# Statistics of two RMSNorms as split float32r matmuls in a hybrid decoder layer

## The chip, the cores and the metric

The kernel runs on one core of one Trainium2 chip. The metric is the time of one launch in device microseconds (us). Before the change it is 837.26 us, the median of 3 runs (836.93 to 837.74).

## The reference

One decoder layer on 512 tokens of width 1024: a half-step SwiGLU feed-forward, a mixer (RG-LRU channels beside sliding-window attention), and a second half-step feed-forward. Each of the three is wrapped in an RMSNorm on its input (pre norm) and one on its output (post norm):

```python
def rms_norm(x, g):
    xf = x.astype(jnp.float32)
    y = xf * lax.rsqrt(jnp.mean(xf * xf, axis=-1, keepdims=True) + RMS_EPS)
    return (y * g.astype(jnp.float32)).astype(x.dtype)

x = x + 0.5 * rms_norm(swiglu(rms_norm(x, ffn1_pre_g), ffn1_w_gu, ffn1_w_down), ffn1_post_g)
y = hybrid_mixer(rms_norm(x, mix_pre_g), w_in, ...)
x = x + rms_norm(y, mix_post_g)
x = x + 0.5 * rms_norm(swiglu(rms_norm(x, ffn2_pre_g), ffn2_w_gu, ffn2_w_down), ffn2_post_g)
```

All inputs are float32. The change touches the pre norms with `mix_pre_g` and `ffn2_pre_g`: the mean over 1024 features of the squares, for each of the 512 tokens.

## The kernel before, in words

**Layout.** x lies feature-major: 8 tiles `xT[c]` of 128 features by 512 tokens. Every large product is made of float32r matmuls (a form of fp32 that the array takes as one matmul record; the trace prints its type as fp32r where an engine writes it). Since float32r keeps fewer bits, each operand is split in a high part (a rounded copy made by ACT) and a low part (what is left, a subtraction on DVE), and each product is three matmuls: high by high, high by low, low by high (`mm3`, L509).

**A pre norm.** The class `Next` (L635) prepares the input of the next product. The gain is multiplied in before the product; the factor 1/rms of each token is multiplied in after it, so the product need not wait for the statistics. `sum_squares` (L653) adds the squares of the 8 tiles into `acc` (128 by 512): ACT squares (L656, L658 through `square`, L542), DVE adds (L658). `stats` (L582) then needs, for each token, the sum of `acc` over 128 partitions times 1/1024. It takes four matmuls, one for each block of 128 tokens, with the block of `acc` as the stationary operand and a column `mean_d` of 1/1024 as the moving one, in plain fp32 (L585); the result is one column per block. `invert` (L588) takes the root on ACT (L592), the reciprocal on DVE (L593), and lays the reciprocals on the diagonals of two tiles, high and low (L594 to L598). `spread` (L600) multiplies them with a matrix of ones (L602) so that every partition has 1/rms of every token, and ACT copies the result to the tile R (L666).

**Where it stands in the order.** The order on all engines is written out by hand: each engine runs its instructions in the order of the program. `boundary` (L755) ends one sub-layer and starts the next. Near its end stand `W.fill(2)`, `nxt.sum_squares()` (L825), and then the rest of the first four weight blocks' matmuls (`k_high`, L826, and `k_low`, L827). After `boundary` comes the next product, `pk` for the mixer (L1565) and `pg` of chunk 2 for the second feed-forward (L1111): 24 matmuls, and after 12 of them (the hook at k = 4) the `stats` matmuls. `spread` comes behind the product.

**Weights.** A queue (`Weights`, L50) loads raw weights over SP's DMA queue, rounds them on ACT (`cast`, L210) and subtracts on DVE or POOL (`take_low`, L215), a few units ahead of their use; a raw buffer that both have read is loaded again.

**Buffers.** Scratch tiles from `wt` (L163) share a ring of 8 buffers, `acc` tiles a ring of 3, PSUM has 8 banks in turn. A ring's buffer is used again when its last reader is done.

**Who else uses `InvRmsRows`.** The norm of the LRU output (`lrms`, L1895) and, through a subclass, the first layer's pre norm.

Of the kernel before, what the change touches and what calls it, by code (L numbers as in the profile page):

```python
# [8 lines left out]
F32 = mybir.dt.float32  # L9
F32R = mybir.dt.float32r  # L10
# [5 lines left out]
P = 128  # L16
T = 512
NB = T // P
D = 1024
# [103 lines left out]
def tile_layer(ctx: ExitStack, tc: tile.TileContext, out: bass.AP, **ins: bass.AP):  # L123
    nc = tc.nc
    pe, dve, act, pool, sync = nc.tensor, nc.vector, nc.scalar, nc.gpsimd, nc.sync

    const = ctx.enter_context(tc.tile_pool(name="const", bufs=1))
# [14 lines left out]
    def bank(name):  # L142
        return psum.tile([P, T], F32, tag="bank", name=name)
# [19 lines left out]
    def wt(name, w=T, dt=F32):  # L163
        return tmp.tile([P, w], dt, tag="w", name=name, bufs=NW)
# [291 lines left out]
    for name, n in ROWS:  # L456
        if name in ("b_rg", "b_ig"):

            j = name == "b_ig"
# [14 lines left out]
    def filled(name, w, value):  # L474
        t = const.tile([P, w], F32, name=name)
        dve.memset(t, value)
        return t
# [2 lines left out]
    dve.memset(ones.bitcast(F32), 1.0)  # L480
    mean_d = filled("mean_d", 1, 1.0 / D)
    mean_c = filled("mean_c", 1, 1.0 / C)
    eps = filled("eps", 1, EPS)
    eps4 = filled("eps4", 1, 4 * EPS)
    dummy = const.tile([P, 1], F32, name="dummy")
# [30 lines left out]
    def product(w, xs, sl=ALL, name="", hooks=()):  # L516
        ps = bank(name)
        hooks = dict(hooks)
        for k, x in enumerate(xs):
            if k in hooks:  # L520
                hooks[k]()
            mm3(ps[:, sl], w, k, [t[:, sl] for t in x], k == 0, k == len(xs) - 1)
        return ps
# [16 lines left out]
    def square(src, sl, name, scale=1.0):  # L540
        sq = wt(f"sq_{name}")[:, sl]
        act.activation(sq, src, AF.Square, scale=scale)  # L542
        return sq
# [3 lines left out]
    class InvRms:  # L547


        def __init__(self, accs, mean, half, name, eps=eps):  # L550
            self.accs, self.mean, self.half, self.name, self.eps = accs, mean, half, name, eps

        def stats(self):
            self.ps = ps = bank(f"rms_{self.name}")
            for i in range(2):
                b = 2 * self.half + i
                for j, a in enumerate(self.accs):
                    pe.matmul(ps[:, i:i + 1], a[:, b * P:(b + 1) * P], self.mean, start=j == 0, stop=j == len(self.accs) - 1)
            self.invert(ps[:, :2])
# [16 lines left out]
    class InvRmsRows:  # L576


        def __init__(self, acc, mean, name):
            self.acc, self.mean, self.name = acc, mean, name  # L580

        def stats(self):  # L582
            self.ps = ps = bank(f"rms_{self.name}")
            for b in range(NB):
                pe.matmul(ps[:, b:b + 1], self.acc[:, b * P:(b + 1) * P], self.mean, start=True, stop=True)  # L585
            self.invert(ps[:, :NB])
# [48 lines left out]
    class Next:  # L635
# [17 lines left out]
        def sum_squares(self):  # L653
            for c in range(KD):
                if c == 0:
                    act.activation(self.acc, xT[c], AF.Square)  # L656
                else:
                    dve.tensor_add(self.acc, self.acc, square(xT[c], ALL, f"n{self.name}{c}"))  # L658

        def stats(self):  # L660
            self.rms.stats()
# [802 lines left out]
    for g, (f0, f1) in enumerate(GROUPS1):  # L1464
# [20 lines left out]
        for c in range(KD):  # L1485
# [18 lines left out]
            b = pair_banks[c] if c < 2 else product(W.take(), xs, name=f"ya{g}{c}")  # L1504
# [6 lines left out]
    def in_product(name, hooks=(), ahead=AHEAD):  # L1511
        return product(W.take(ahead), mx.xs, name=name, hooks=hooks)
# [81 lines left out]
    for j in range(4):  # L1594
        b = in_product(f"pq{j}")
# [70 lines left out]
    hl = us_  # L1666
# [473 lines left out]
```

## Time and profile before

| | before |
|---|---|
| median of 3 runs | 837.26 us |
| the profiled execution | 837.42 us |
| its span, first to last instruction | 835.6 us |
| granted TensorE clock | 0.998 |
| busy: PE / PEld / DVE / ACT / POOL | 827.5 / 704.3 / 732.7 / 518.8 / 165.9 us |

PE is TensorE's matmuls, PEld its weight loads, which overlap the matmuls; DVE is VectorE, ACT ScalarE, POOL GpSimd, SP the queue that issues DMAs. A record's end on PE is modelled, and records overlap: the step from one start to the next tells more than the length. In a row of the timeline stand the start, the length, the engine, the line, the operation, output and inputs, the shape, how many records were merged, and in brackets how long the engine idled before and who ended that. In a matmul's row "128*128 128x512" is the stationary shape and the moving shape.

### The profile page before, as it was taken

The numbers are of one execution on the slowest core, as the hardware profiler recorded it, in microseconds if no ns is written. First come the engines' busy times: TensorE is split into PE (matmuls) and PEld (weight loads), VectorE is DVE, ScalarE is ACT, GpSimd is POOL, SyncE is SP. The second block draws the span as 40 slices with busy tenths as digits, with TensorE's granted clock in tenths as the row PEclk, the third lists the DMA queues.
The fourth block names the chain that finished last, engine by engine and source line by source line (L and its number), as shares of the span: only waits on it lengthen the run. The fifth ranks groups of instructions, "written<-read, shape, count | busy, mean of one in ns | idle before, by whom it ended". The sixth has DMA issues, their size and how long they took to land.

```text
span 835.6 us, 11875 instructions
## 1 busy us (share of the span) xinstructions
PE 827.5 (99%) x4244; PEld 704.3 (84%) x4244; DVE 732.7 (88%) x1035; ACT 518.8 (62%) x806; POOL 165.9 (20%) x188
## 2 busy tenths in 40 slices
PE   9999999999999999999999999999999999999996
PEld 8988888888888898987788899888888888888885
DVE  4989799998989977888789689998999799898996
ACT  6656756676666654556897446545757677676562
POOL 2022000140320325414521052002005023032001
PEclk9999999999999999999999999999999999999999
DMA  7376408398595897522511140566339939769742
GB/s 253 103 272 231 151 12 308 89 266 259 128 260 179 187 282 244 170 79 93 167 42 51 51 130 23 126 176 253 118 110 243 311 91 256 234 156 259 301 141 101
DMA packets 121851, 144.22 MB, mean 173 GB/s; under 512 B 24184, under 2 KB 76736, under 8 KB 121280
## 3 DMA queue, kind: packets, MB, share of 16 engines
q1 hardware_dynamic: 107824, 112.91, 42.2%
q0 software_dynamic: 13824, 30.42, 16.6%
q8 instruction: 33, 0.54, 0.3%
q14 instruction: 26, 0.21, 0.1%
q10 hardware_dynamic: 144, 0.13, 0.0%
HBM read 100.45 MB, written 39.32 MB: 167 GB/s over the span
## 4 chain that ended last, share of the span: by engine, by line
PE 98%; DMA 1%; DVE 0%; SPq 0%; issue 0%; DVEq 0%
PE aa L999 10%; PE ab L999 10%; PE db L999 5%; PE da L999 5%; PE yaa L1390 3%; PE ba L999 3%; PE bb L999 3%; PE ya L1390 3%; PE yda L1390 2%; PE aa L929 1%; PE a_first L1260 1%; PE yab L1981 1%; PE yab L1979 1%; PE yab L1980 1%; PE wo L1905 1%; PE gt L512 1%
## 5 line engine op out<-in xcount | busy, mean ns | idle before, releaser
L1171 POOL DMA_DIRECT2D yr_a<-stage x36 | 31.6, 1020 | 176.5 <-ACT stage L1168 156.0
L1171 POOL DMA_DIRECT2D yp_b<-stage x42 | 36.5, 1065 | 146.8 <-ACT stage L1168 118.4
L1995 POOL DMA_DIRECT2D yp_b<-stage x8 | 4.3, 546 | 64.9 <-ACT stage L1994 64.4
L722 POOL TENSOR_TENSOR acca_r<-acca_r,sq_r 128x512 f32<-128x512 f32 x6 | 8.6, 1430 | 39.7 <-ACT sq_r L542 39.6
L530 PE MATMUL an<-xh_mx,whi_xl 128*128 128x256 f32 x64 | 15.9, 289 | 0.0
L531 PE MATMUL an<-xh_mx,wlo_xl 128*128 128x256 f32 x64 | 15.5, 283 | 0.0
L2098 POOL TENSOR_TENSOR last<-yp,grow 128x512 f32<-128x512 f32 x3 | 3.9, 1292 | 56.5 <-DVE yp L2088 56.5
L2095 ACT ACTIVATE ysq<-yp 128x512 f32<-128x512 f32 (+1 forms) x8 | 4.9, 607 | 15.7 <-DVE yp L2088 15.7
L512 PE MATMUL gt<-xh_mx,whi_gt 128*128 128x512 f32 x32 | 14.3, 446 | 0.0
L1427 POOL DMA_DIRECT2D yp_a<-zy x16 | 8.7, 554 | 25.0 <-DMA rows_a<-yr_a 16.7
L512 PE MATMUL pq<-xh_mx,whi_q 128*128 128x512 f32 x32 | 12.8, 401 | 0.0
L514 PE MATMUL gt<-xh_mx,wlo_gt 128*128 128x512 f32 x32 | 12.6, 394 | 0.0
L512 PE MATMUL pgb<-xh_f,whi_bg 128*128 128x512 f32 x32 | 12.6, 393 | 0.0
L513 PE MATMUL gt<-xl_mx,whi_gt 128*128 128x512 f32 x32 | 12.5, 391 | 0.0
L514 PE MATMUL pq<-xh_mx,wlo_q 128*128 128x512 f32 x32 | 12.5, 391 | 0.0
L514 PE MATMUL pgb<-xh_f,wlo_bg 128*128 128x512 f32 x32 | 12.5, 390 | 0.0
L514 PE MATMUL pub<-xh_f,wlo_bu 128*128 128x512 f32 x32 | 12.5, 390 | 0.0
L513 PE MATMUL pq<-xl_mx,whi_q 128*128 128x512 f32 x32 | 12.5, 390 | 0.0
L513 PE MATMUL pub<-xl_f,whi_bu 128*128 128x512 f32 x32 | 12.5, 390 | 0.0
L512 PE MATMUL pub<-xh_f,whi_bu 128*128 128x512 f32 x32 | 12.5, 390 | 0.0
L513 PE MATMUL pgb<-xl_f,whi_bg 128*128 128x512 f32 x32 | 12.5, 389 | 0.0
L1390 PE MATMUL ya<-whi_ad,hha 128*128 128x512 f32 x32 | 12.5, 389 | 0.0
(2038 smaller groups left out, 3414.3 us busy)
## 6 DMA issues: line engine op xcount, KB each, us to landing
yp_b<-stage POOLq DMA_DIRECT2D x50, 256.0 KB, 9.0
yr_a<-stage POOLq DMA_DIRECT2D x44, 256.0 KB, 9.6
h_a<-za SPq DMA_DIRECT2D x16, 256.0 KB
h_b<-zb SPq DMA_DIRECT2D x16, 256.0 KB
hxb<-h_b SPq DMA_DIRECT2D x16, 256.0 KB
hxa<-h_a SPq DMA_DIRECT2D x6, 512.0 KB
xn<-in_x SPq DMA_DIRECT2D x8, 256.0 KB
raw_ad<-in_ffn_w_down SPq DMA_DIRECT2D x2, 1024.0 KB
```

The lines of the kernel that those rows point to most:

```text
L512: pe.matmul(ps, hi[:, k, :], xh, start=start, stop=False)
L513: pe.matmul(ps, hi[:, k, :], xl, start=False, stop=False)
L514: pe.matmul(ps, lo[:, k, :], xh, start=False, stop=stop)
L530: pe.matmul(ps[:, sl], hi[:, k, :], xh, start=k == 0 and not goes_on, stop=False, skip_group_check=True)
L531: pe.matmul(ps[:, sl], lo[:, k, :], xh, start=False, stop=False, skip_group_check=True)
L722: eng.tensor_add(acc, acc, square(part, ALL, f"{self.name}{c}"))
L929: pe.matmul(o, w[:, k, js], x, start=first and i + j + k == 0, stop=k == 3 and i == 2, skip_group_check=True)
L999: pe.matmul(b[tb], x[:, blk], w[:, k, :], start=first and q + k + j == 0, stop=q + k == 2 and j == 2, skip_group_check=True)
L1171: pool.dma_start(o, st, accum_op=ALU.add)
L1260: pe.matmul(banks[j][:, HALF[0]], ws[j][part][:, k, :], n1.xs[k][xpart][:, HALF[0]], start=k == 0 and part == xpart, stop=stop and k == KD ...
L1390: pe.matmul(o, x[:, blk], a[:, k, :], start=start and j == 0, stop=stop and j == 2, skip_group_check=True)
L1427: (pool if q % 2 else sync).dma_start(chunks[32 * q:32 * (q + 1), :, i * P:(i + 1) * P], turned[32 * i:32 * (i + 1), :, q])
```

## The change

The sum of squares of the two pre norms gets a method `apart`, called at the end of `sum_squares`: ACT copies `acc` to a float32r tile (the high part) and DVE subtracts it from `acc` (the low part), both in tiles of the `wt` ring. `stats` then takes, for each block of 128 tokens, two float32r matmuls (high, then low, added in PSUM) with two equal columns of 1/1024 in place of one fp32 matmul with one column. The root reads every second column. The LRU norm and the first pre norm keep the old way. `mean_r` is a new constant of two columns, set once at the start.

```diff
     mean_d = filled("mean_d", 1, 1.0 / D)
     mean_c = filled("mean_c", 1, 1.0 / C)
+    mean_r = const.tile([P, 2], F32R, name="mean_r")
+    dve.memset(mean_r.bitcast(F32), 1.0 / D)
...
         def __init__(self, acc, mean, name):
-            self.acc, self.mean, self.name = acc, mean, name
+            self.acc, self.mean, self.name, self.two = acc, mean, name, None
+
+        def apart(self):
+
+            self.two = hi, lo = [wt(f"acc{i}_{self.name}", T, F32R) for i in "hl"]
+            act.copy(hi, self.acc)
+            dve.tensor_sub(lo, self.acc, hi.bitcast(F32))
 
         def stats(self):
             self.ps = ps = bank(f"rms_{self.name}")
+            if self.two:
+                for b in range(NB):
+                    for j, a in enumerate(self.two):
+                        pe.matmul(ps[:, 2 * b:2 * b + 2], a[:, b * P:(b + 1) * P], mean_r, start=j == 0, stop=j == 1)
+                self.invert(ps[:, 0:2 * NB:2])
+                return
             for b in range(NB):
                 pe.matmul(ps[:, b:b + 1], self.acc[:, b * P:(b + 1) * P], self.mean, start=True, stop=True)
             self.invert(ps[:, :NB])
...
                     dve.tensor_add(self.acc, self.acc, square(xT[c], ALL, f"n{self.name}{c}"))
+            self.rms.apart()
```

## The prediction

> **What bounds the kernel now.** I read the busy times first, then the chain that ended last, then the waits of PE.
>
> ```profile
> PE 827.5 (99%) x4244; PEld 704.3 (84%) x4244; DVE 732.7 (88%) x1035; ACT 518.8 (62%) x806; POOL 165.9 (20%) x188
> ...
> PE 98%; DMA 1%; DVE 0%; SPq 0%; issue 0%; DVEq 0%
> ```
>
> ```profile
> PE warm L1247 <- POOL ident masks.py:199: 1.4, 1, 1.4
> PE xtp L1195 <- DMA xn<-in_x: 0.4, 1, 0.4
> ```
>
> PE is busy for 827.5 of 835.6 us, the chain of work that ended last is PE for 98%, and PE's whole list of waits is 1.8 us at the start. So PE never waits in the two stages that the change touches. Time can change in two ways only: the statistics' own records on PE get cheaper or dearer, or a wait of PE appears where there is none. What ACT and DVE do more is free as long as PE finds its data.
>
> **The statistics on PE now.** The timeline of PE and of its weight loads around the mixer's statistics, and the records of line 585:
>
> ```profile
> 365.81 0.39 PE L512 MATMUL pk<-xh_mx,whi_kv 128*128 128x512 f32 x1
> ...
> 368.30 0.39 PE L514 MATMUL pk<-xh_mx,wlo_kv 128*128 128x512 f32 x1
> 368.53 0.95 PE L585 MATMUL rms_nmx<-mean_d,acc_nmx 128*128 128x1 f32 x8
> 369.34 0.49 PE L512 MATMUL pk<-xh_mx,whi_kv 128*128 128x512 f32 x1
> 369.66 0.40 PE L513 MATMUL pk<-xl_mx,whi_kv 128*128 128x512 f32 x1
> ```
>
> ```profile
> 368.31 0.19 PEld L585 LDWEIGHTS rms_nmx<-mean_d,acc_nmx 128*128 128x128 f32 x1
> ...
> 369.31 0.19 PEld L512 LDWEIGHTS pk<-xh_mx,whi_kv 128*128 128x128 f32 x1
> 369.42 0.19 PEld L513 LDWEIGHTS pk<-xl_mx,whi_kv 128*128 128x128 f32 x1
> ```
>
> ```profile
> L585 PEld LDWEIGHTS rms_nmx<-mean_d,acc_nmx x8: 188/192/192, 368.3 to 369.2; 128*128 128x128 f32 x8
> L585 PE MATMUL rms_nmx<-mean_d,acc_nmx x8: 164/250/251, 368.5 to 369.2; 128*128 128x1 f32 x8
> ```
>
> The reader is to see three things. First, four matmuls in the program stand as 8 pairs of weight load and matmul in the trace: an fp32 matmul is two pairs. Second, what they cost. In the run of 512-column matmuls the step is (368.30 - 365.81) / 11 = 0.226 us. From 368.30 to 369.66 it takes 1.36 us for what would be two steps (0.45), so the statistics cost 0.91 us. Third, why. A load starts when the matmul before it starts, because only then is the spare weight buffer free. With one column there is no stream to hide it behind, and the loads stand end to end: the second starts at 368.53 (as the first statistics matmul starts), the load of the next product at 369.31, seven steps later, 0.111 us each. The eight steps from 368.53 to 369.42, where the load of L513 begins and so the matmul of L512 truly starts, are 0.89 us: the whole cost but 0.02 us. So **a pair costs its load, 0.111 us; its columns cost nothing.**
>
> **The new statistics on PE.** Four blocks times two parts: 8 float32r matmuls for 8 fp32 pairs, each with a 128 by 128 load. One float32r matmul is one pair: 12 of them stand as 12 records between 365.81 and 368.30. The trace has no float32r matmul under 256 columns, so the cost of one with two columns is bounded from rows. The nearest row is a load: L512's at 369.31 follows the statistics, has nothing to hide behind, and the next float32r load starts at 369.42, so a bare float32r load takes 0.11 us, the same as an fp32 one. The nearest matmuls are the 256-column ones:
>
> ```profile
> 353.73 0.28 PE L530 MATMUL an<-xh_mx,whi_xl 128*128 128x256 f32 x1
> ...
> 358.41 0.28 PE L531 MATMUL an<-xh_mx,wlo_xl 128*128 128x256 f32 x1
> ```
>
> They take 4.68 / 39 = 0.120 us a step, and the columns set that (halving 512 to 256 took off 0.106, so 0.0135 is left for no columns). With two stages there are 16 pairs. At 0.111 the change is 0; at 0.120 it is 16 x 0.009 = +0.14 us; at the step of a 512-column matmul, an estimate from afar, 16 x (0.226 - 0.111) = +1.85 us; if they cost nothing at all, -16 x 0.111 = -1.78 us. I take 0.111, since the load is the one part that a two-column pair shares with both forms: **sum on PE 0.0 us**, and keep -1.8 and +1.85 as the ends.
>
> By the Trainium skill, "FP8 and Floating Point Precision" (TensorE Precision Notes), a true fp32 matmul is four passes and a reduced one is one; counted in passes, 16 passes a stage become 8, and the sum would be half of 0.89 off in each stage, -0.9 us. The trace shows two records and not four for each fp32 matmul, and at one column it is the loads that take the time, so the sum does not use it.
>
> **The second stage** is the same by its rows; I use the f2 statistics only for the timing of the neighbours, below.
>
> **What ACT and DVE add, mixer.** The copy is 128x512 fp32 to fp32r on ACT, the subtraction the same shape on DVE:
>
> ```profile
> 373.35 0.62 ACT L1368 CAST gates<-gates_raw 128x512 fp32r<-128x512 f32 x1
> ```
>
> ```profile
> 543.91 0.68 DVE L695 TENSOR_TENSOR b2l_f<-xb_f,b2h_f 128x512 fp32r<-128x512 f32 x1
> ```
>
> ```profile
> 360.69 5.71 DVE L658 TENSOR_TENSOR acc_nmx<-acc_nmx,sq_nmx 128x512 f32<-128x512 f32 x7
> 366.42 1.23 DVE L215 TENSOR_TENSOR wlo_q<-raw_q,whi_q 128x1024 fp32r<-128x1024 f32 x1
> 369.81 0.18 DVE L593 RECIPROCAL rs_nmx<-rms_nmx 128x4 f32<-128x4 f32 x1 [2.17 <-ACT rms_nmx L592]
> ```
>
> ```profile
> 365.33 1.05 ACT L210 CAST whi_q<-raw_q 128x1024 fp32r<-128x1024 f32 x1 [4.61 <-PE an L537]
> 369.51 0.26 ACT L592 ACTIVATE rms_nmx<-rms_nmx,eps 128x4 f32<-128x4 f32 x1 [3.13 <-PE rms_nmx L585]
> ```
>
> The last addition ends at 360.69 + 5.71 = 366.40. A handover between ACT and DVE takes 0.04 us (root ends 369.77, reciprocal starts 369.81). So the copy runs 366.44 to 367.06 and the subtraction 367.10 to 367.78. PE loads the first high block at 368.31 and the first low one at 368.53: slack 1.25 and 0.75 us. This is the cover, 12 matmuls of `pk` between the sums and the statistics; every us beyond it would be a us of the total.
>
> Queued behind the new wait: on ACT the rounding of whi_q, now at 365.33, which then runs 367.06 to 368.11; on DVE the subtraction wlo_q, which needs it and runs 368.15 to 369.38. Both engines are free again before the root (369.51) and the reciprocal (369.81). Nothing behind them moves. wlo_q is first used by the products two further on. The two new scratch tiles push the ring on by two, so for eight tiles the buffer in question was freed two tiles later than before; those are squares that were added up by 366.40 and the new tiles themselves, read by 369.3, while their next users come later (POOL's mask tile at about 364 in place of 362.31, with 10 us of idle time behind it):
>
> ```profile
> 362.31 1.16 POOL L1379 TENSOR_SCALAR_AFFINE_SELECT upf<-home 128x512 f32<-128x512 f32 x1 [7.69 <-DVE acc_nmx L658]
> ...
> 374.06 1.30 POOL L1369 TENSOR_TENSOR gates<-gates_raw,gates 128x512 fp32r<-128x512 f32 x1 [10.01 <-ACT gates L1368]
> ```
>
> **The same, second feed-forward.** Here the engines behind have less air:
>
> ```profile
> 517.77 5.46 DVE L658 TENSOR_TENSOR acc_nf<-acc_nf,sq_nf 128x512 f32<-128x512 f32 x7
> 523.49 1.23 DVE L215 TENSOR_TENSOR wlo_bg<-raw_bg__4971,whi_bg 128x1024 fp32r<-128x1024 f32 x1 [0.25 <-ACT whi_bg L210]
> 524.63 1.22 DVE L215 TENSOR_TENSOR wlo_bu<-raw_bu__5062,whi_bu 128x1024 fp32r<-128x1024 f32 x1
> 526.88 0.18 DVE L593 RECIPROCAL rs_nf<-rms_nf 128x4 f32<-128x4 f32 x1 [1.03 <-ACT rms_nf L592]
> ...
> 527.99 0.68 DVE L598 TENSOR_TENSOR dl_nf<-ident,rl_nf 128x512 fp32r<-128x512 f32 x1
> ```
>
> ```profile
> 522.40 1.05 ACT L210 CAST whi_bg<-raw_bg__4971 128x1024 fp32r<-128x1024 f32 x1 [4.60 <-PE mn L537]
> 523.36 1.04 ACT L210 CAST whi_bu<-raw_bu__5062 128x1024 fp32r<-128x1024 f32 x1
> 524.31 1.04 ACT L210 CAST whi_bg<-raw_bg__5385 128x1024 fp32r<-128x1024 f32 x1
> 526.59 0.26 ACT L592 ACTIVATE rms_nf<-rms_nf,eps 128x4 f32<-128x4 f32 x1 [1.23 <-PE rms_nf L585]
> ```
>
> ```profile
> 529.52 0.39 PE L602 MATMUL rms_nf<-dl_nf,ones 128*128 128x512 f32 x1
> ```
>
> ```profile
> 525.60 0.95 PE L585 MATMUL rms_nf<-mean_d,acc_nf 128*128 128x1 f32 x8
> ```
>
> The additions end at 523.23; copy 523.27 to 523.89, subtraction 523.93 to 524.61, PE's matmuls start at 525.60: slack about 1.0 us. The three roundings behind the copy move from 522.40 to 523.89, at their steps of 0.95, and the last ends at about 526.8, so the root starts 0.2 late. On DVE wlo_bg runs 524.9 to 526.15, wlo_bu to 527.28, and the reciprocal is 0.3 to 0.4 late. Then dl, which ended at 528.67, ends at about 529.07. PE reads it at 529.52: **slack 0.45 us**, the smallest of the change. After this DVE has no idle time for 40 us, so it stays 0.4 us late that long:
>
> ```profile
> 526.88:567.67 40.79, 40.79 (x182) 33.68 (x181) 40.29 (x68) 20.14 (x29) 0.00 (x0) 1.00 0.67 170
> ```
>
> ```profile
> 541.04 1.22 DVE L215 TENSOR_TENSOR wlo_bg<-raw_bg__5385,whi_bg 128x1024 fp32r<-128x1024 f32 x1
> ...
> 568.08 0.69 DVE L855 TENSOR_TENSOR u<-pub,R_f 128x512 f32<-128x512 f32 x1 [0.41 <-PE pub L514]
> ```
>
> ```profile
> 546.57 0.39 PE L514 MATMUL pgb<-xh_f,wlo_bg 128*128 128x512 f32 x1
> ```
>
> PE first wants something of that stretch at 546.57, the wlo_bg that DVE ends at 542.26: slack 4.3 us against 0.4. At 568.08 DVE waits for PE and has made the delay good. The raw weights that are loaded after these subtractions start 1.4 us later on SP's queue, which the same slack covers. Setting `mean_r` at the start is one more DVE write of a few bytes before PE has any data: 0.
>
> **Sum.** PE 0.0, ACT and DVE hidden, no new wait: 837.42 us of the profiled execution stays 837.42. That execution stood 0.16 above the median of 837.26; I forecast **837.3 us**. A measurement of this kernel can tell about 0.2%, 1.67 us, from no change.
>
> **The rivals.**
> *A pair in float32r is cheaper than one in fp32.* For it: one pass in place of several. Against it: the loads at 369.31 and 369.42. At half price it is -0.9 us, 836.4; at a quarter, 16 x 0.083 = -1.3, 836.0; hidden wholly, 835.5, the one case below the 0.2% bound. The Trainium skill, "TensorE: Matmul & The Clock Gate" (Weight-path perf modes), has a fast weight load, four chunks at once, for 128 weights whose type is not fp32; if that held for float32r it would be the quarter case. The float32r loads of 0.11 us speak against it.
> *PE waits.* If copy, rounding and subtraction come later than worked out by over 0.45 us, the spread matmul in the second feed-forward is late first, then the mixer's low part at 0.75. The price is what is over; with 0.7 us more in each stage, 0.25 + 0, with a whole subtraction and copy more, 1.3 us, about 0.85 + 0.55. I put it at up to +1.0, 838.3.
> *Slower: the pairs do not overlap.* High and low add into the same two columns, and if the second had to see the first one out of the array, each pair would cost a matmul's length, 0.250 us by the row of line 585, in place of 0.111: 16 x 0.139 = +2.2, 839.5 (+0.27%). It decides from a step of 0.215 us a pair. Against it: the 8 fp32 records add in the same way and overlap at 0.111.
> *Not what it says:* a float32r matmul of so few columns could be run as fp32, two pairs each: 16 more pairs, +1.78, 839.1 (+0.21%). Nothing in the trace is that narrow, which is all that speaks for it.
>
> **Chances.** Forecast 0.62; half price 0.08; quarter 0.04; free 0.04; PE waits 0.08; no overlap 0.08; as fp32 0.06. Slower by over 0.2% is the last two, 0.14; faster only the free case, 0.04; within 0.2% 0.82. The range leaves out the free, the quarter and the no-overlap case (0.16) and takes in the fp32 case: 836.0 to 839.2 us with the runs' own spread.
>
> **What would show it.** In the timeline of PE after, 8 records of the statistics between two `pk` matmuls with a step of 0.11, and 1.36 us from the matmul before to the second one behind: that is the 0. A step of 0.03 or 0.055 is the first rival, 0.25 the third, 16 records the fourth. PE's list of waits should still hold only the start; an entry at L602 or at the statistics is the second. On DVE the reciprocal of the second feed-forward should come 0.3 to 0.4 us after the root's old place allows, that of the mixer unchanged. The forecast is wrong if PE's step at two columns is not that of its load.

## The result, and the profile after

The change makes the kernel slower: 841.08 us against 837.47 us (medians of 4 runs each), ratio 1.0045 with a 95% interval of 1.0033 to 1.0058, some 3.6 us. The profiled execution has a span of 838.6 us against 835.6. I had forecast 837.3 us and a range to 839.2.

First the place that I had worked on. The timeline of PE of the changed kernel around the mixer's statistics (start, length, engine, line, operation):

```profile
367.97 0.39 PE L514 MATMUL pk<-xh_mx,whi_kv 128*128 128x512 f32 x1
...
370.46 0.40 PE L516 MATMUL pk<-xh_mx,wlo_kv 128*128 128x512 f32 x1
370.70 0.16 PE L595 MATMUL rms_nmx<-mean_r,acch_nmx 128*128 128x2 f32 x1
370.73 0.25 PE L595 MATMUL rms_nmx<-mean_r,accl_nmx 128*128 128x2 f32 x1
370.84 0.25 PE L595 MATMUL rms_nmx<-mean_r,acch_nmx 128*128 128x2 f32 x1
...
371.40 0.25 PE L595 MATMUL rms_nmx<-mean_r,accl_nmx 128*128 128x2 f32 x1
371.51 0.48 PE L514 MATMUL pk<-xh_mx,whi_kv 128*128 128x512 f32 x1
371.82 0.39 PE L515 MATMUL pk<-xl_mx,whi_kv 128*128 128x512 f32 x1
```

Eight records, a step of 0.11 us (only the first is shorter), and 371.82 - 370.46 = 1.36 us from the matmul before to the second one behind: to the hundredth what it was. The statistics cost nothing more and nothing less. DVE in the same stage:

```profile
369.29 0.69 DVE L588 TENSOR_TENSOR accl_nmx<-acc_nmx,acch_nmx 128x512 fp32r<-128x512 f32 x1 [0.74 <-ACT acch_nmx L587]
370.25 1.23 DVE L215 TENSOR_TENSOR wlo_q<-raw_q,whi_q 128x1024 fp32r<-128x1024 f32 x1 [0.26 <-ACT whi_q L210]
371.98 0.18 DVE L607 RECIPROCAL rs_nmx<-rms_nmx 128x4 f32<-128x4 f32 x1 [0.51 <-ACT rms_nmx L606]
```

The subtraction ends at 369.98, 0.72 before PE's first narrow matmul, and the reciprocal starts 1.28 us after that matmul, as before (369.81 - 368.53).

But all these rows stand 2.2 us later than their counterparts: the first `pk` matmul was at 365.81 and is at 367.97. The second statistics stand 1.7 us later (527.31 for 525.60), so nothing is lost between the two places. **Most of the time was lost before the first changed instruction on PE.** PE's waits of the changed kernel say where:

```profile
PE warm L1262 <- POOL ident masks.py:199: 1.4, 1, 1.4
PE ya L514 <- ACT hha L951: 1.1, 1, 1.1
PE ydb L1996 <- DVE hla L897: 0.7, 1, 0.7
PE ya L515 <- DVE hla L883: 0.4, 1, 0.4
...
```

In the timeline of PE they stand here:

```profile
312.39 0.50 PE L515 MATMUL ya<-hla,whi_ad 128*128 128x512 f32 x1 [0.41 <-DVE hla L883]
314.97 0.50 PE L514 MATMUL ya<-hha,whi_ad 128*128 128x512 f32 x1 [1.15 <-ACT hha L951]
...
804.75 0.50 PE L1996 MATMUL ydb<-whi_bdu__7824,hla 128*128 128x512 f32 x1 [0.69 <-DVE hla L897]
```

The two waits at `ya` are at the end of the first feed-forward, the wait at `ydb` is near the end of the second. Behind the first pair stands DVE, which adds up and turns the row sums that come back from HBM. The timeline of DVE, first of the kernel before, then of the changed one (in brackets the idle time and who ended it):

```profile
301.58 1.35 DVE L1418 STREAM_TRANSPOSE zy<-rows_a 128x512 f32<-128x512 f32 x2 [1.03 <-DMA rows_a<-yr_a]
302.92 0.69 DVE L1417 TENSOR_TENSOR rows_a<-rows_a,yda 128x512 f32<-128x512 f32 x1
```

```profile
302.66 1.40 DVE L1433 STREAM_TRANSPOSE zy<-rows_a 128x512 f32<-128x512 f32 x2 [2.34 <-DMA rows_a<-yr_a]
305.61 0.69 DVE L1432 TENSOR_TENSOR rows_a<-rows_a,yda 128x512 f32<-128x512 f32 x1 [1.55 <-DMA rows_a<-yr_a]
```

DVE starts on the first row sum 1.1 us later, and for the third one it now waits again, so that its addition starts 2.7 us later. The transfer that both wait for has the same code in both kernels. Its issues on SP (shortest, median and longest in ns, before and after) are not alike:

```profile
L1408 SPq DMA_DIRECT2D rows_a<-yr_a x8: 319/320/793, 292.2 to 301.6; - x8
```

```profile
L1423 SPq DMA_DIRECT2D rows_a<-yr_a x8: 319/436/2425, 292.3 to 302.7; - x8
```

The longest, 2.43 us, is the first of the eight, which took 0.32 us before. The table of DMA queues, before and after:

```profile
q1 hardware_dynamic: 107824, 112.91, 42.2%
q0 software_dynamic: 13824, 30.42, 16.6%
```

```profile
q1 hardware_dynamic: 107824, 112.91, 43.0%
q0 software_dynamic: 13824, 30.42, 17.2%
```

Packets and bytes are equal to the last one, but they took a larger share of a longer span: 60.2% of 838.6 us against 58.8% of 835.6, 2.7% more DMA time. So the reader is to look for something that makes the same packets slower. Sorted by size, the records of the packets show which ones (the median of the 512-byte packets of q1; of the 2 KB packets of q0, which add the partial sums to rows in HBM, the mean and how many of the 9984 took over 250 ns):

```
                 512 B, median   2 KB adding, mean   over 250 ns
before                27 ns            176.9 ns           23
after                 33 ns            183.5 ns          170
```

The 512-byte packets are of several kinds. The 16384 that take the hidden values out of the z buffers go from 32 to 34 ns in the median, the 4096 that load `w_in` into raw weight buffers from 27 to 31; the median of all mixes them.

One thing of the change touches all transfers: where the buffers lie. In the built programs a constant of a few columns takes 32 bytes per partition, and the constants of the kernel before end exactly at 18432 = 36 x 512, where the layer tiles (t2k, R, z) begin, and behind them the weights. `mean_r` is one constant more. With it all large buffers start at 18464, 32 bytes off.

### The profile page after: what moved, and what is told of

It is laid out like the page before. It is cut to its first block, busy times and chain, and to the rows that moved or that the text cites. A ratio compares the mean times of both kernels' runs of the same rounds, so it can differ in the third digit from the quotient of the medians.

```text
span 838.6 us, 11883 instructions
## 1 busy us (share of the span) xinstructions
PE 828.1 (99%) x4244; PEld 703.3 (84%) x4244; DVE 732.2 (87%) x1038; ACT 516.2 (62%) x808; POOL 166.9 (20%) x188
## 3 DMA queue, kind: packets, MB, share of 16 engines
q0 software_dynamic: 13824, 30.42, 17.2%
## 4 chain that ended last, share of the span: by engine, by line
PE 89%; DVE 4%; DMA 4%; issue 1%; ACT 1%; SPq 0%; DVEq 0%; POOL 0%; ACTq 0%; POOLq 0%
PE aa L1014 10%; PE ab L1014 9%; PE da L1014 5%; PE db L1014 5%; PE yaa L1405 3%; PE ya L1405 3%; PE ba L1014 3%; PE bb L1014 2%; PE yda L1405 2%; PE a_first L1275 1%; DMA rows_a<-yr_a 1%; PE wo L1920 1%; DMA hxa<-h_a 1%; PE yab L1994 1%; PE yab L1995 1%
## 5 line engine op out<-in xcount | busy, mean ns | idle before, releaser
L514 PE MATMUL ya<-hha,whi_ad 128*128 128x512 f32 x30 | 11.8, 394 | 1.1 <-ACT hha L951 1.1
```

The source lines that it names most:

```text
L514: pe.matmul(ps, hi[:, k, :], xh, start=start, stop=False)
```

## The experiments

**Place or work.** Theory A: the 32 bytes of the constant. Theory B: the copy, the subtraction and the narrow matmuls. e1 is the kernel before with the constant alone, e2 the change without it:

```diff
     mean_c = filled("mean_c", 1, 1.0 / C)
+    unused = filled("unused", 2, 1.0 / D)          # e1, on the kernel before
```

```diff
-    mean_d = filled("mean_d", 1, 1.0 / D)
+    mean_r = const.tile([P, 2], F32R, name="mean_r")      # e2, on the change
+    dve.memset(mean_r.bitcast(F32), 1.0 / D)
+    mean_d = mean_r.bitcast(F32)[:, 0:1]
```

> The kernel before with one unused constant of two columns and nothing else: no split, no float32r statistics. It moves the start of every large buffer by 32 bytes per partition (18432 to 18464), as the change does. Theory A (the place: the constant shifts all buffers off their 512-byte starts and the transfers get slower): the time of the change, +3 to +4 us on before, ratio 1.0035 to 1.005. Theory B (the work: copy, subtraction and narrow matmuls): the time of before, ratio 1.000 +- 0.001. Theory C (neither, the transfers' times differ from run to run or chip to chip): before.

> The whole change, but the one-column constant is taken as the first column of the two-column one, so that no 32 bytes are added and every large buffer starts where it did before (18432). Theory A: the time of before, ratio 1.000 +- 0.001 (my step by step sum of 0.0 us then holds). Theory B: the time of the change, +3 to +4 us, ratio 1.0035 to 1.005. A mix of both would show as something between, and with e1 adding up to the change.

Measured: e1 843.5 us, ratio 1.0070 (1.0051 to 1.0088), more than the 1.0035 to 1.005 that I had expected; e2 837.32 us, ratio 0.9997 (0.9988 to 1.0006). Eight bytes that nobody reads cost all of the loss; the whole change without them costs nothing. PE's waits of e1, then of e2:

```profile
PE warm L1248 <- POOL ident masks.py:199: 1.4, 1, 1.4
PE ya L513 <- ACT hha L937: 1.1, 1, 1.1
PE ydb L1982 <- DVE hla L883: 1.0, 1, 1.0
PE ab L1000 <- ACT bb L1005: 1.0, 1, 1.0
PE yaa L1391 <- ACT stage L1169: 0.6, 1, 0.6
...
```

```profile
PE warm L1262 <- POOL ident masks.py:199: 1.4, 1, 1.4
PE xtp L1210 <- DMA xn<-in_x: 0.3, 1, 0.3
```

e1, which computes just what the kernel before does, has the waits of the changed kernel at `ya` and `ydb` and two more; e2 has only those of the start. The runs of e1 lie between 839.85 and 845.77, those of e2 between 836.9 and 837.96: with the shift the times scatter more too, and e1's being 2.4 us above the change is within that. Theory B falls.

**How large the unit is.** The change with more unused constants, so that the buffers start 64, 128 or 256 bytes off:

```diff
+    unused = filled("unused", 2, 0.0)     # e3: 64 bytes off in all; 24 columns in e5: 128; 56 in e4: 256
```

> The whole change with one more unused constant: the large buffers start at 18496, a multiple of 64 but not of 128. Theory A with a 64-byte unit: back to before, ratio 1.000 +- 0.001, and 512-byte packets back at their length of before. Theory A with a larger unit: as the change, ratio 1.003 to 1.005. Theory B: as the change.

> The whole change with 96 more bytes of unused constant: the large buffers start at 18560, a multiple of 128 but not of 256. If the unit is 256 bytes: 512-byte packets at 33 ns, the time of the change, ratio 1.003 to 1.006. If the unit is 128 bytes: packets at 27 ns and the time of before, 1.000 +- 0.001.

> The whole change with 224 more bytes of unused constant: the large buffers start at 18688, a multiple of 256 but not of 512. Theory A with a unit of 64 to 256 bytes: back to before, ratio 1.000 +- 0.001. Theory A with a unit of 512: as the change, 1.003 to 1.005. Theory B: as the change.

Measured: 64 bytes 841.01 us, 1.0043 (1.0028 to 1.0057); 128 bytes 837.72 us, 1.0008 (0.9999 to 1.0016); 256 bytes 837.18 us, 0.9997 (0.9989 to 1.0006). The packets:

```
shift          512 B, median   2 KB adding, mean   over 250 ns
 32 (e1)            33 ns            184.8 ns          181
 64 (e3)            33 ns            182.4 ns          137
128 (e5)            34 ns            177.0 ns           19
256 (e4)            27 ns            176.6 ns           15
```

The length of a 512-byte packet has a unit of 256 bytes, as one of my expectations for e5 had it; the adding packets are disturbed at 32 and 64 bytes only, and so is the median time of the kernel. So the forecast for e5 held for the packets and failed for the time. But the execution of e5 that was profiled, from which its row of the table is taken, is the slowest of its 11: 839.8 us (another took 839.12, the other nine 837.2 to 838.0). PE's waits in it:

```profile
PE warm L1263 <- POOL ident masks.py:199: 1.4, 1, 1.4
PE xtp L1211 <- DMA xn<-in_x: 0.9, 2, 0.5
PE ydb L1997 <- DVE hla L898: 0.7, 1, 0.7
PE ya L515 <- ACT hha L952: 0.5, 1, 0.5
```

PE waits at `ya` and `ydb` here too, with no more long adding packets (19) than before. At 128 bytes the loss is mostly absent, not always, and long adding packets are not needed for it.

**Which buffers.** From here on the constant is shared as in e2, and the shifts are set by hand. e6 shifts the layer tiles alone, e7 weights and scratch alone, e8 the two z buffers alone (through a longer R tile ahead of them, in both lines that make one); in e6 and e8 a gap behind the layer tiles, 224 bytes, puts the weights at a shift of 256:

```diff
+    unused = filled("unused", 2, 0.0)                                   # e6, and a gap of 56 columns
+    big.tile([P, 8], F32, tag="gap", name="gap")                        # e7
-        return big.tile([P, T], F32, tag="R", name=name)
+        return big.tile([P, T + 8], F32, tag="R", name=name)[:, :T]     # e8, and a gap of 56 columns
```

> The whole change with the constant shared; then 32 bytes are put ahead of the pool of layer tiles alone (t2k, R, z), and 224 behind it, so that weights and scratch start at 256-byte multiples as good as before. Theory A1 (transfers out of and into the layer tiles are the slow ones, the weights' loads are not): nearly all of the loss, 1.003 to 1.007. Theory A2 (the weights' loads, the most bytes): 1.000 +- 0.001.

> The other way round: the layer tiles stay where they are, 32 bytes are put behind them, so that raw weights, rounded weights, acc tiles and scratch are shifted by 32 bytes. Theory A1: 1.000 +- 0.001, 512-byte packets at 27 ns. Theory A2: 1.003 to 1.007.

> Only the two wide z buffers are shifted by 32 bytes, all else sits at 256-byte multiples as before. They are what the turned hidden values and the turned row sums are sent out of in 512-byte pieces, and what they are read back into. If these small pieces are what counts: most 512-byte packets at 33 ns, the 128-byte ones and the accumulating ones as before, and 1.002 to 1.005. If the accumulating transfers of the stage tiles count (they are 2 KB each): 1.000 +- 0.001 here.

Measured: e6 853.88 us, 1.0202 (1.0189 to 1.0216); e7 854.36 us, 1.0205 (1.0192 to 1.0218); e8 843.26 us, 1.0065 (1.0052 to 1.0077). e8 gives the whole loss with the z buffers alone. e6 and e7 are 17 us slower, which neither theory had: I had changed a second thing. The chain of work in the first feed-forward, start, length and records of one product, before and in e7:

```profile
189.80 5.44 PE ba L999 x24
```

```profile
194.46 5.60 PE ba L1014 x24
```

The same 24 matmuls take 5.60 in place of 5.44 us, a step of 0.2333 us in place of 0.2267, from the first feed-forward to the last. In all kernels up to e5 the weights and the layer tiles had been shifted together; in e6 and e7 PE's two operands stand 224 and 32 bytes apart. So the times of e6 and e7 say nothing on their question. Their adding packets do: 163 take over 250 ns in e6, whose layer tiles are shifted, and 20 in e7, whose weights are. In e8, which shifts no operand of the great products, the mean step over the kernel is 0.227, as in the kernel before.

**Out of z or into it.** The z buffers are made 128 bytes longer, so that they start at 0 and at 128, and the transfers of one direction alone start 32 bytes into them. e9: the turned hidden values and turned row sums that are read out; e10: the hidden values and sums that are written in.

```diff
-        return big.tile([P, NB * T], F32, tag="z", name=name, bufs=2)
+        return big.tile([P, NB * T + 32], F32, tag="z", name=name, bufs=2)[:, off:off + NB * T]
...
-            z = wide(f"z{n}")
+            z = wide(f"z{n}", 8)                                 # e9, and "zy0"; in e10 "hx" and "yp_a"
```

> All buffers at multiples of 128 bytes (each z buffer is 128 bytes longer); only the transfers that read the z buffers (turned hidden values to HBM, turned row sums to their new places) read 32 bytes into them. If the loss comes from reading the small pieces at 32 bytes: ratio 1.004 to 1.007 as with both directions off (e8), and the accumulating packets at 183 to 185 ns in the mean. If it comes from writing into the z buffers: 1.000 to 1.001, as at a shift of 128.

> The counterpart: only the transfers that write into the z buffers (hidden values fetched back, the moved row sums) start 32 bytes into them. If writes off a 128-byte start are what costs (they leave parts of lines to be merged): 1.004 to 1.007 and the long accumulating packets. If reads cost: 1.000 to 1.001.

Measured: e9 842.8 us, 1.0059 (1.0047 to 1.0072); e10 837.3 us, 0.9999 (0.9990 to 1.0008). Reads alone give the loss. (In the built programs the hidden values are always fetched back into the second z buffer, so in e10 those writes start at 128 + 32 = 160 bytes; hidden values written at 32 were moved only in e8, which is no slower than e9 beyond the intervals.) The profile's record of the row sums' issue on SP (shortest, median and longest in ns), in e9 and in e10, and PE's waits of e9:

```profile
L1423 SPq DMA_DIRECT2D rows_a<-yr_a x8: 320/594/2960, 294.7 to 305.4; - x8
```

```profile
L1423 SPq DMA_DIRECT2D rows_a<-yr_a x8: 319/320/740, 293.2 to 302.3; - x8
```

```profile
...
PE ya L514 <- ACT hha L951: 1.2, 1, 1.2
PE ydb L1996 <- DVE hla L897: 1.1, 1, 1.1
PE ab L1014 <- ACT bb L1019: 0.8, 1, 0.8
PE yaa L1405 <- ACT stage L1183: 0.8, 1, 0.8
```

With reads 32 bytes off, SP itself is held up at the row sums for up to 2.96 us, and 156 adding packets take over 250 ns; with the writes moved, 0.74 us and 17 packets. The waits of e9 are those of e1, place by place. SP's first issue of the row sums takes 2.4 to 3.5 us in every kernel that reads z 32 or 64 bytes off (the change, e1, e3, e6, e8, e9) and 0.32 in all others.

Which reads? The records of the long adding packets say it by their times: in e9 153 of the 156, in the change 165 of the 170 start within 10 us of an issue of the hidden values (`h_a<-za`, `h_b<-zb`), stretches that hold only some 1500 of the 9984. No run shifts the hidden values apart from the first half of the row sums.

**The weights' loads, and PE's step.** Two questions were open: whether the loads of the weights, the most bytes, have a share, and what the second effect is. e13 shifts the raw buffers alone (a gap of 32 bytes ahead of them, one of 224 behind); e11, e16, e12, e14 and e15 are e7 with 64, 96, 128, 192 and 224 bytes.

```diff
+    big.tile([P, 16], F32, tag="gap", name="gap")       # e11; 24 in e16, 32 in e12, 48 in e14, 56 in e15
+    wpool.tile([P, 56], F32, tag="gap2", name="gap2")   # e13, behind the raw buffers, with 8 columns ahead
```

> Only the five raw weight buffers start 32 bytes off (layer tiles, rounded weights and scratch at 256-byte multiples), so PE's operands keep their offset: step 0.2267. If the weights' loads count for the loss: 1.002 to 1.005. If the reads out of the z buffers are all of it, as e8 and e9 against e10 say: 1.000 to 1.001 (half of the moved row sums are read out of a raw buffer, so a trace of the loss may stay).

> As e7, but weights and scratch shifted by 64 bytes in place of 32, the layer tiles unmoved. In e7 PE itself was slower, 0.2333 us a step of a 512-column matmul in place of 0.2267, where stationary and moving operand stand 32 bytes apart. If that is a matter of 64-byte units: step 0.2267 and a time near before, 1.000 to 1.002. If any offset between the two does it: 1.02 as e7. The weights' loads are then off a 128-byte start too; if they counted for the loss as the z buffers do, 1.003 to 1.007 with a step of 0.2267.

> 96 bytes, between 0.2301 (64) and 0.2324 (128): a step of 0.2333 as at 32 if what counts is the parity of 32-byte units, about 0.231 if it changes evenly; 1.008 to 1.020.

> The same with 128 bytes. If PE's step depends on the offset in units of 64 or 128 bytes: 0.2267 and 1.000 +- 0.002. If it depends on the offset within 256 bytes or more: another step than 0.2267, slower as in e7 or, if the present offset is not the best one, faster; each 0.0011 us a step would be about 2.5 us of the whole.

> Weights 192 bytes off against the layer tiles. If PE's step depends on the offset between its two operands within 256 bytes and is the same both ways: as 64 bytes, 0.2301, 1.007 to 1.009. If the present offset 0 is not the best: a step under 0.2267 and a faster kernel, each 0.0011 us about 2.5 us. If the slower step of e7, e11 and e12 had another cause (the gap behind the layer tiles): something else than these.

> 224 bytes. Same both ways: as 32 bytes, step 0.2333, 1.020. Offset 0 not the best: under 0.2267 and faster than before.

Measured: e13 837.06 us, 0.9997 (0.9988 to 1.0005): the loads have no share in the loss, though their 512-byte packets, those of `w_in`, take 32 ns in place of 27; its adding packets are at 176.8 ns. Nor has the second half of the row sums, which is read out of a raw buffer. For the others, with the mean step between 512-column matmuls from the timeline's starts:

```
weights off by   kernel   time, us   ratio (interval)            step, us
  0              e2        837.32    0.9997 (0.9988 to 1.0006)    0.2269
 32              e7        854.36    1.0205 (1.0192 to 1.0218)    0.2333
 64              e11       843.69    1.0088 (1.0072 to 1.0104)    0.2301
 96              e16       854.77    1.0208 (1.0195 to 1.0222)    0.2335
128              e12       852.56    1.0181 (1.0167 to 1.0194)    0.2324
192              e14       850.96    1.0162 (1.0148 to 1.0176)    0.2323
224              e15       853.18    1.0190 (1.0176 to 1.0204)    0.2333
```

The step does depend on the offset between PE's operands: some 2900 such steps at 0.0064 us more are 18.6 us, and e7 is 17.2 us slower. The 256-column matmuls give some back, for they go the other way: the median of their step is 0.120 us at 0, 0.117 at 32 and 0.114 at 64. The odd multiples of 32 are all at 0.2333 to 0.2335, and for 512 columns 0 is the best of those tried. My guess for e14, that 192 would be like 64 the other way round, failed. No version beat the kernel before; e2 and e4, the change with the buffers on their lines, equal it.

## Why the prediction was wrong

**What held.** The sum that I made holds as it stands, but for a kernel with the buffers where they were: e2 is the change with nothing shifted, and its 0.9997 is the 0.0 us that I forecast. A float32r pair of two columns costs its load, 0.11 us by the rows above; the rivals with cheaper pairs, pairs that do not overlap and two pairs each would have shown steps of 0.03 or 0.055, 0.25 or 16 records, and none did. The fast weight load, which the Trainium skill, "TensorE: Matmul & The Clock Gate" (Weight-path perf modes), has for types other than fp32, is not seen for float32r here: the bare loads still stand 0.11 us apart. The times of ACT and DVE came out within 0.1 us of those worked out. In the second feed-forward, DVE of the changed kernel:

```profile
527.78 1.22 DVE L215 TENSOR_TENSOR wlo_bu<-raw_bu__5072,whi_bu 128x1024 fp32r<-128x1024 f32 x1
528.92 0.17 DVE L607 RECIPROCAL rs_nf<-rms_nf 128x4 f32<-128x4 f32 x1
```

The reciprocal starts 1.61 us after PE's first statistics matmul (527.31) in place of 1.28, so 0.33 us late, where I had said 0.3 to 0.4, and PE did not wait at the spread.

**What failed** is one step: "Setting `mean_r` at the start is one more DVE write of a few bytes before PE has any data: 0." I counted the write of the constant and not its place. Its 32 bytes push every buffer behind it off its 256-byte line. What the runs put there: +3.6 us in the change, +6.0 in e1 (843.5 - 837.47), seen in the profile as waits of PE (1.1, 0.4 and 0.7 us in the change), the first two of them behind transfers that the diff does not touch. My first paragraph had said that a new wait of PE is one of the two ways in which time can change; I then looked for one only in the two stages with new code. But for the constant the diff had no edit outside them, and still a wait came at 312 us, in the sub-layer before.

The rule that would have spoken against the change was at hand. The Trainium skill, "DMA: Bandwidth & Descriptors" (How a descriptor splits into AXI transactions), says that a transaction starts on a 256-byte line, so a descriptor that does not gets one transaction more. The 512-byte packets that read the hidden values agree: in the median 32 ns at shifts of 0 and 256, 34 to 35 at 32 and 64, 38 at 128. By that page alone 128 bytes should be as bad as 32 or worse, since more of each line is fetched unused; the kernel's time at 128 bytes, 1.0008, does not agree, but for two of its eleven executions.

**The chain, as far as it is shown.** Reads out of the z buffers that start 32 bytes off make the loss (e8, e9); the writes that e10 moved and the weights' loads do not (e10, e13). In every kernel with such reads at 32 or 64 bytes 137 to 191 of the adding packets take over 250 ns, in every other 30 or fewer. SP's first issue for the row sums is held up, DVE gets and turns them late, and PE waits at `ya`. That the long adding packets make the row sums themselves late is not shown: in the changed kernel the last of the first feed-forward's adding transfers lands at 299.68 us, in the kernel before at 299.61. **What stays open:** what holds SP up; why reads off a line disturb the adding packets at 32 and 64 bytes and not at 128; what made two executions of e5 lose time all the same; and what makes DVE late before the wait at `ydb`. No run tells the possible causes apart.

## What to carry to other kernels

Ask of every new tile where it lies, not only what it costs: a constant ahead of the large pools moves all of them, so compare the buffers' start addresses of the two programs, modulo 256, before reading a diff as local. If the time is lost before the first changed instruction, run the kernel before with the new allocation alone; one such run settles it. Put a small constant into a slot that exists, or fill up to the next 256 bytes.

## What the runs showed of the hardware

A 512-byte packet that is read out of a z buffer takes 32 ns in the median when its buffer starts on a 256-byte line, 34 to 35 when it starts 32 or 64 bytes off and 38 at 128; one that is loaded into a raw buffer, 27 on the line and 29 to 32 off it. Reads out of the z buffers 32 or 64 bytes off make other transfers slower: the 2 KB packets that add into HBM rise from 177 to between 182 and 185 ns in the mean, through 137 to 191 packets that take over 250 ns, the longest 2.7 us (e9), in place of 176 ns.

PE's step for a 512-column float32r matmul with a new stationary block depends on the offset between the stationary and the moving operand in the partition: 0.227 us at 0 or 256 bytes, 0.230 at 64, 0.232 at 128 and 192, 0.233 at the odd multiples of 32 that were tried (32, 96, 224). In a kernel that PE bounds this was worth up to 2%, nearly five times the loss under study. The step of a 256-column one falls, from 0.120 at 0 to 0.114 at 64 (medians). Why the offset matters no run tested.
